# One layer of attention and state-space mixing on one core: scores over the whole array with k held twice, q's norm factor in the exponential, another order of panels

## Chip, core and metric

The kernel runs on one core of a Trainium2 chip. The metric is the device time of one execution in microseconds (us). Before the change the median of three runs is 595.13 us (594.83 to 597.0).

## What is computed

One layer of a decoder for 256 tokens of width 1024, in float32. The input is normed and multiplied with one wide matrix; its columns feed an attention branch (q, k, v, 16 heads of 64) and a state-space branch (z, xBC, dt), each gated (g_a, g_b). A gated feed-forward part and a small last gate follow.

```
h  = rms_norm(x, ln1_g)
proj = h @ w_in
q, k, v, z, xbc, dt_raw, gate_a, gate_b = jnp.split(proj, IN_OFFSETS, axis=-1)
qh = rms_norm(split_heads(q, b_, s), q_norm_g)
kh = rms_norm(split_heads(k, b_, s), k_norm_g)
att = moba_attention(qh, kh, split_heads(v, b_, s))
y_a = att @ w_o_attn
y_b = mamba2_mixer(z, xbc, dt_raw, ...) @ w_o_ssm
x = x + (sigmoid(gate_a) * y_a + sigmoid(gate_b) * y_b) @ w_out
g_ff, u_ff = jnp.split(rms_norm(x, ln2_g) @ w_gate_up, 2, axis=-1)
x = x + (silu(g_ff) * u_ff) @ w_down
x = x + (p @ w_ple_proj) * sigmoid(rms_norm(x, ln3_g) @ w_ple_gate)
```

With 256 tokens there is one attention block, so the attention is plain causal attention: the scores of a head are q times k over 64 dimensions, divided by 8, masked and put through a softmax. q and k are normed per head and token before that: each row is multiplied by a factor (its mean square plus epsilon, to the power -1/2) and by a gain per dimension.

## The kernel before

**Precision.** Every large product is done on TensorE in a rounded float32. Each factor is split into a rounded high part and the rest; three products (high x high, high x low, low x high) add up in PSUM. Names ending in h and l are such pairs.

**Weights.** The matrices come as one stream of 512 KB pieces. `load` (L271) starts the DMA into `raw` (5 buffers) on SP's queue, ACT rounds the piece into `wh` (4 buffers, L151), and DVE subtracts for `wl` (6 buffers, L265). L151 is a helper: all of ACT's work has this line, all matmuls have L170, all transposes L192.

**Panels.** The stream is used up in the order of the list `PANELS` (L34): each entry is 512 output columns. A `Panel` (L335; v, q, k, gb, ga, yb) has the tokens as output rows, takes two PSUM banks (`g`) and 48 products of 128x512. `Rows` (L380; xbc) and `Narrow` (L404; z) have the columns as output rows and take four banks (`gr`, pairs of a 128x512 and a 128x256 product) and two (`gn`, 96 products of 128x256). Panels share four banks of PSUM; a panel's first product into a bank waits until ACT or DVE have read what stood there. The first two panels (v) run while the input arrives; v, q and k use an input pair made at the start (`split_h`), and from `gb` on the panels use `hn`, which `norm_task` (L463) makes in four steps of two rows each on DVE and ACT (L486).

**Side tasks.** All else (transposes, scores, values, convolutions, the scan) runs between the panels' products. Tasks are generators; a `Filler` (L78) walks them as the panels are written out: after each step of a panel it lets one task that is due emit its next piece. When a task is due is told in a planner's own time by the table `LAG` (L68), in nanoseconds. So `PANELS` and `LAG` set where each piece stands in TensorE's order, and with it when the other engines are asked. Side tasks share four other banks of PSUM (`pb`).

**q and k** (`evac_qk`, L630). For each of the panel's two banks (128 tokens each) ACT squares, DVE sums per head (L640) and adds epsilon (L642), POOL raises both to -1/2 (L644), and DVE multiplies the bank by the factor into SBUF (L647), which frees it. After the delay `qk`, TensorE transposes, ACT multiplies by the gain and rounds, and DVE makes the low part (L658). The result has two heads on each block of 128 partitions.

**Scores** (`scores`, L837) take a pair of heads, eight pairs in all. Each head's product runs over its 64 partitions alone, and `halves` (L176) writes the two heads in turn, as they use different halves of the array's rows. There are twelve products a pair: for each head three of 128 columns (first 128 queries, first 128 keys) and three of 256 (the other queries, all keys). DVE adds the mask and takes the maximum, ACT takes the exponential with a scale of 0.125 and the maximum as bias, and DVE divides by the sum. `transp` (L871) transposes the probabilities, `values` (L887) multiplies them with v for two pairs at a time, always those before the newest.

Of the kernel before, what the change touches and what calls it, by code (L numbers as in the profile page):

```python
# [16 lines left out]
P = 128  # L17
T = 256
# [6 lines left out]
V_CW = 26  # L25
# [30 lines left out]
    ('ga', 1, 8736),
# [12 lines left out]
    "norm": 7560, "norm.x": 1763, "norm.k": 4255, "dt": 4000, "dt.t": 3068, "dt.e": 21098, "dt.low": 0,  # L69
    "dt.end": 1000, "xbc": 3513, "xbc.t": 2655, "xbc.end": 16932, "z": 9234, "z.t": 0, "z.end": 2000,  # L70
    "qk": 30613, "qk.t": 841, "qk.end": 1559, "v": 3285, "cb": 0, "rows": 0, "prep": 1025, "seg": 263,
    "seg.next": 4000, "out": 3075, "out.xdt": 2489, "out.end": 1108, "off": 2201, "off.end": 1168,
    "finish": 5045, "finish.ones": 8043, "sc": 0, "sc.tr": 0, "tr": 802, "tr.val": 0, "val": 1761, "val.end": 0,
    "m": 1896, "res": 7162, "ff": 609, "ff.end": 7593,
# [34 lines left out]
def tile_layer(ctx: ExitStack, tc: tile.TileContext, head, xk, pt, vec, w_dt, w_big, w_dn2, w_pp, out):  # L109
# [23 lines left out]
    def s4(shape, dt=F32):  # L133
        return sb.tile([P] + shape, dt, tag="s4", bufs=22, name=nm("s4"))
# [304 lines left out]
    eps1 = const.tile([P, 2], F32, name="eps1")  # L439

    def x_stats():
        with prio("bg"):
# [11 lines left out]
            nc.vector.tensor_scalar(eps1, ss1s, EPS / 1024, EPS * EPS, op0=ALU.mult, op1=ALU.add)  # L454

# [173 lines left out]

    def evac_qk(kind, i, pan):  # L630
        gcol = v[:, V_GQ : V_GQ + 1] if kind == "q" else v[:, V_GK : V_GK + 1]
        th = s4([4, T], F32R)
        tl = s4([4, T], F32R)
        qn = []
        with prio("ev"):
            ms = tiny([2, 8])
            for tt in range(2):
                sqr = s2([512])
                act(sqr, pan.ps[tt], AF.Square)
                nc.vector.tensor_reduce(ms[:, tt], sqr.rearrange("p (h d) -> p h d", d=64), axis=AX.X, op=ALU.add)  # L640
            for tt in range(2):
                nc.vector.tensor_scalar(ms[:, tt], ms[:, tt], 1.0 / 64, eps1[:, tt : tt + 1], op0=ALU.mult, op1=ALU.add)  # L642
            f = tiny([2, 8])
            nc.gpsimd.tensor_tensor(f.rearrange("p a b -> p (a b)"), ms.rearrange("p a b -> p (a b)"), mhalf, op=ALU.pow)  # L644
            for tt in range(2):
                q_ = s2([512])
                nc.vector.tensor_tensor(  # L647
                    q_.rearrange("p (h d) -> p h d", d=64), pan.ps[tt].rearrange("p (h d) -> p h d", d=64), bcast(f[:, tt], 64), op=ALU.mult)
                qn.append(q_)
        yield fill.now + LAG["qk"]  # L650
        for tt in range(2):
            with prio("bg"):
                pq = pb([4, P])
                for j in range(4):
                    transpose(pq[:, j], qn[tt][:, j * P : j * P + P])
                ts = slice(tt * P, tt * P + P)
                act(th[:, :, ts], pq, scale=gcol)
                stt(tl[:, :, ts], pq, gcol, th[:, :, ts].bitcast(F32), op0=ALU.mult, op1=ALU.subtract)  # L658
            yield fill.now + LAG["qk.t"]
        yield fill.now + LAG["qk.end"]  # L660
        qk_t[kind, i] = (th, tl)
# [171 lines left out]
    def attention_task():  # L833
# [3 lines left out]
        def scores(p):  # L837
            half, i = p
            (qh, ql), (kh, kl) = qk_t["q", half], qk_t["k", half]
            with prio("bg"):  # L840
# [3 lines left out]
                ps = [pb([512]) for _ in range(2)]  # L844
                halves(
                    (ps[hf][:, o], a[rows_of[hf], i, qs], b[rows_of[hf], i, ks], n == 0, n == 2)
                    for o, qs, ks in ((slice(0, P), slice(0, P), slice(0, P)), (slice(P, P + T), slice(P, T), slice(0, T)))
                    for n, (a, b) in enumerate(((qh, kh), (qh, kl), (ql, kh)))
                    for hf in range(2))
                for hf in range(2):  # L850
                    p_ = ps[hf]
                    nc.vector.tensor_tensor_reduce(
                        out=s[:, hf, 0:P], in0=p_[:, 0:P], in1=cmask[:, 1], scale=1.0, scalar=-3.0e38,
                        op0=ALU.add, op1=ALU.max, accum_out=mx[:, 2 * hf : 2 * hf + 1])
                    nc.vector.tensor_tensor_reduce(
                        out=s[:, hf, P : P + T], in0=p_[:, P : P + T], in1=cmask.rearrange("p a b -> p (a b)"), scale=1.0, scalar=-3.0e38,
                        op0=ALU.add, op1=ALU.max, accum_out=mx[:, 2 * hf + 1 : 2 * hf + 2])
# [295 lines left out]
def _layout(i):  # L1153
# [9 lines left out]
    def chunks(w, c0, k0, nk):  # L1163
# [5 lines left out]
        np.concatenate([f["q_norm_g"]] * 2)[:, None], np.concatenate([f["k_norm_g"]] * 2)[:, None],  # L1169
# [55 lines left out]
```

## Time and profile before

| | before |
|---|---|
| median of three runs | 595.13 us |
| the profiled execution | 595.48 us |
| its span, first to last instruction | 593.8 us |
| mean granted clock of TensorE | 0.999 |
| products on TensorE (PE) | 3183 |
| DMA traffic | 104.97 MB, mean 177 GB/s |

The profile is of one execution. A line of its tables names the source line, the engine, the operation and output <- inputs by the program's names; the shapes are partitions x elements, and for a matmul the size of the weights and of the moving rows. A timeline row starts with the start time and the time busy, both in us; brackets hold the idle time ahead of it on its engine and the instruction that ended it. Products are pipelined: one row's end lies behind the next row's start, so the cost of a product is the distance of starts. A count at the end (x12) joins equal rows that follow each other. In a row of groups the first number behind the bar is the busy time of all, the second the mean of one in ns, then the idle time ahead of them.

### The profile page before, as it was taken

The page shows a single profiled execution, that of the slowest core. Times are in us where ns is not written, and L with a number is a line of the kernel's source. Part 1 is how long each engine was busy: PE and PEld are TensorE (multiplying, and loading weights), DVE is VectorE, ACT ScalarE, POOL GpSimd, SP SyncE. Part 2 cuts the span into 40 slices and gives each one's busy share as a digit, 9 for nine tenths or more (in the row PEclk, how much of TensorE's full clock was granted, in tenths as well). Part 3 has the DMA queues.
Part 4 walks back from the last instruction along what each step waited for, and adds up shares of the span by engine and source line. Part 5 has one row for each costly group of instructions (what it writes and reads, how often), then busy time and mean ns, then how long its engine had stood idle before and what let it go on. Part 6 is the DMA issues. An engine that isn't in the chain of part 4 may idle for free.

```text
span 593.8 us, 8655 instructions
## 1 busy us (share of the span) xinstructions
PE 585.2 (99%) x3183; PEld 493.4 (83%) x3183; DVE 439.8 (74%) x703; ACT 340.9 (57%) x528; POOL 38.7 (7%) x44
## 2 busy tenths in 40 slices
PE   8999999999999999999999999999999999999997
PEld 7787778888899889888888888888888888888886
DVE  5696787999889999997957766666656666646464
ACT  6874566776877757655643445755445545445352
POOL 2004231000000024100000000000000000000000
PEclk9999999999999999999999999999999999999999
DMA  8957548655443333344465675555665565556521
GB/s 271 386 179 235 169 161 218 202 174 166 151 160 104 108 109 85 131 159 162 142 228 182 191 247 184 192 170 186 194 196 175 179 198 189 180 191 193 182 73 71
DMA packets 33322, 104.97 MB, mean 177 GB/s; under 512 B 3616, under 2 KB 7040, under 8 KB 33280
## 3 DMA queue, kind: packets, MB, share of 16 engines
q1 hardware_dynamic: 33280, 104.43, 54.1%
q8 instruction: 25, 0.41, 0.3%
q14 instruction: 17, 0.14, 0.1%
HBM read 103.28 MB, written 1.06 MB: 176 GB/s over the span
## 4 chain that ended last, share of the span: by engine, by line
PE 93%; ACT 2%; DMA 2%; DVE 1%; POOL 1%; issue 1%; SPq 1%; ACTq 0%
PE g L170 64%; PE gr L170 10%; PE gn L170 8%; PE pb L170 6%; PE pb L192 4%; ACT wh L151 1%; DMA raw<-in_head 1%; DMA xraw<-in_head 1%; ACT s L151 1%; POOL tiny L644 1%; DVE wl L265 1%; SPq L250 1%; DVE s L647 0%; DVE tiny L640 0%; DVE tiny L642 0%
## 5 line engine op out<-in xcount | busy, mean ns | idle before, releaser
L170 PE MATMUL g<-wh,s 128*128 128x512 f32 (+1 forms) x1188 | 374.6, 392 | 1.2 <-ACT wh L151 0.7
L265 DVE TENSOR_TENSOR wl<-raw,wh 128x1024 fp32r<-128x1024 f32 (+2 forms) x193 | 231.0, 1200 | 113.4 <-ACT wh L151 111.0
L151 ACT ACTIVATE wh<-raw 128x1024 fp32r<-128x1024 f32 (+2 forms) x193 | 200.1, 1038 | 179.6 <-PE g L170 131.1
L170 PEld LDWEIGHTS g<-wh,s 128*128 128x128 f32 x1188 | 222.5, 188 | 47.1 <-ACT wh L151 1.1
L170 PE MATMUL g<-wl,s 128*128 128x512 f32 (+1 forms) x594 | 230.5, 390 | 0.3 <-DVE wl L265 0.3
L170 PEld LDWEIGHTS g<-wl,s 128*128 128x128 f32 x594 | 111.5, 188 | 22.3 <-DVE wl L265 0.9
L170 PE MATMUL gr<-s,wh 128*128 128x512 f32 x192 | 69.1, 401 | 0.9 <-ACT s L151 0.9
L170 PE MATMUL gr<-s,wl 128*128 128x256 f32 x192 | 54.0, 281 | 0.0
L170 PE MATMUL gn<-s,wh 128*128 128x256 f32 x256 | 49.0, 288 | 0.0
L151 ACT ACTIVATE s<-pb 128x512 f32<-128x512 f32 (+3 forms) x58 | 29.0, 531 | 29.2 <-PE pb L192 16.7
L170 PEld LDWEIGHTS gr<-s,wh 128*128 128x128 f32 x192 | 36.0, 188 | 9.5 <-ACT s L151 1.5
L170 PEld LDWEIGHTS gn<-s,wh 128*128 128x128 f32 x256 | 40.2, 191 | 1.0 <-issue 0.3
L170 PE MATMUL gn<-s,wl 128*128 128x256 f32 x128 | 37.0, 289 | 0.0
L170 PEld LDWEIGHTS gr<-s,wl 128*128 128x128 f32 x192 | 36.3, 189 | 0.3
L192 PE MATMUL pb<-ident,s 128*128 128x128 f32 x206 | 33.0, 273 | 0.0
L170 PE MATMUL pb<-s,s 128*64 128x128 f32 (+5 forms) x336 | 30.9, 295 | 0.9 <-ACT s L151 0.9
L600 DVE SCALAR_TENSOR_TENSOR s<-s,vecs,s 128x255 f32<-128x255 f32 (+2 forms) x72 | 31.0, 477 | 0.0
L192 PEld LDWEIGHTS pb<-ident,s 128*128 128x128 f32 x206 | 25.7, 140 | 6.0
L170 PEld LDWEIGHTS pb<-s,s 128*64 128x64 f32 (+2 forms) x336 | 24.4, 158 | 6.7 <-issue 2.2
L710 POOL TENSOR_SCALAR_AFFINE_SELECT rr<-a_h 128x512 fp32r<-128x512 f32 x16 | 16.5, 1045 | 143.9 <-PE pb L170 137.4
L170 PEld LDWEIGHTS gn<-s,wl 128*128 128x128 f32 x128 | 24.4, 191 | 0.4
L151 ACT ACTIVATE s<-s 128x512 f32<-128x512 f32 (+2 forms) x23 | 18.6, 810 | 6.8 <-DVE s L1061 4.0
(143 smaller groups left out, 378.9 us busy)
## 6 DMA issues: line engine op xcount, KB each, us to landing
raw<-in_w_big SPq DMA_DIRECT2D x176, 512.0 KB
raw<-in_head SPq DMA_DIRECT2D x4, 512.0 KB
s<-in_xk SPq DMA_DIRECT2D x4, 512.0 KB
raw<-in_head SPq DMA_DIRECT2D x7, 256.0 KB
e1c<-e1d SPq DMA_DIRECT2D x2, 512.0 KB
raw<-in_w_pp SPq DMA_DIRECT2D x2, 512.0 KB
raw<-in_w_dn SPq DMA_DIRECT2D x2, 512.0 KB
out<-s SPq DMA_DIRECT2D x3, 256.0 KB
```

The costliest lines, as they stand in the source:

```text
L151: return nc.scalar.activation(o, i, f, **kw)
L170: ins = nc.tensor.matmul(o, lhsT, rhs, start=start, stop=stop).ins
L192: queue(nc.tensor.transpose(o, i, ident[: i.shape[0], : i.shape[0]]).ins, False)
L250: nc.sync.dma_start(dst, src)
L265: nc.vector.tensor_sub(wl, raw, wh.bitcast(F32))
L600: stt(cc[:, sft:], u[:, b, : T - sft], cw[3 - sft], cc[:, sft:], op0=ALU.mult, op1=ALU.add)
L644: nc.gpsimd.tensor_tensor(f.rearrange("p a b -> p (a b)"), ms.rearrange("p a b -> p (a b)"), mhalf, op=ALU.pow)
L710: nc.gpsimd.affine_select(r, bcast(a_h[:, c, h0 : h0 + 4].bitcast(F32), P), pattern=[[0, 4], [1, P]], compare_op=ALU.is_ge, fill=0.0, base ...
```

## The change

It has six parts.

**Scores over 128 rows.** k's transposed tiles exist twice. In one copy the 64 partitions of a pair's second head are zero, in the other those of the first, through gains padded with zeros (`vec` has one more column). A product of q's 128 partitions (both heads) with a copy then gives one head alone, and with both copies side by side as moving rows both heads come from one product. A pair takes three products of 256 columns and three of 512 in place of twelve of 128 and 256. They are no longer chained to each other by `halves`.

```diff
-                ps = [pb([512]) for _ in range(2)]
-                halves(
-                    (ps[hf][:, o], a[rows_of[hf], i, qs], b[rows_of[hf], i, ks], n == 0, n == 2)
-                    for o, qs, ks in ((slice(0, P), slice(0, P), slice(0, P)), (slice(P, P + T), slice(P, T), slice(0, T)))
-                    for n, (a, b) in enumerate(((qh, kh), (qh, kl), (ql, kh)))
-                    for hf in range(2))
+                ps = [pb([2, P]), pb([2, T])]
+                for qt in range(2):
+                    for n, (a, b) in enumerate(((qh, kh), (qh, kl), (ql, kh))):
+                        mm(ps[qt], a[:, i, qt * P : qt * P + P], b[:, i % 2, :, : qt * P + P], n == 0, n == 2)
...
-                nc.vector.tensor_scalar(mx, mx, -0.125, None, op0=ALU.mult)
-                parts = (slice(0, P), slice(P, P + T))
+                f = fq[half][:, :, 2 * i : 2 * i + 2]
+                stt(mx.rearrange("p (h q) -> p h q", h=2), mx.rearrange("p (h q) -> p h q", h=2), -1.0, f.rearrange("p q h -> p h q"), op0=ALU.mult, op1=ALU.mult)
...
-                        act(s[:, hf, sl], s[:, hf, sl], AF.Exp, scale=0.125, bias=mx[:, n : n + 1], accum_out=sm[:, n : n + 1])
+                        act(s[:, hf, sl], s[:, hf, sl], AF.Exp, scale=f[:, qt, hf : hf + 1], bias=mx[:, n : n + 1], accum_out=sm[:, n : n + 1])
```

**q's factor in the exponential.** q is not multiplied by its norm factor. ACT copies its banks to SBUF without waiting for POOL, and the factor (with the 1/8 in it, through `eps64`) is the scale of the exponential and multiplies the maximum. k is treated as before up to the transposes, which now take both token blocks of two column blocks at once, sixteen for a panel as before. Behind them k has two evictions on ACT and two on DVE where q has one of each.

```diff
+            if kind == "q":
+                f = fq[i]
+                for tt in range(2):
+                    q_ = s2([512])
+                    act(q_, pan.ps[tt])
+                    qn.append(q_)
...
+                if kind == "q":
+                    outs = [(qh[:, b2], ql[:, b2], V_GQ)]
+                else:
+                    kh, kl = s4([2, 2, T], F32R), s4([2, 2, T], F32R)
+                    kt.append((kh, kl))
+                    outs = [(kh[:, :, hf], kl[:, :, hf], V_GK + hf) for hf in range(2)]
+                for oh, ol, c in outs:
+                    act(oh, pq, scale=v[:, c : c + 1])
+                    stt(ol, pq, v[:, c : c + 1], oh.bitcast(F32), op0=ALU.mult, op1=ALU.subtract)
```

**Buffers.** The pool `s4` of 4 KB tiles has 25 buffers in place of 22.

**Order of panels.** Before: v0 v1 q0 q1 k1 k0 gb0 xbc5 xbc4 xbc1 xbc2 xbc3 xbc0 z0 z1 z2 z3 gb1 yb0 ga0 yb2 ga1 yb1 yb3. Now: v0 v1 k0 q0 q1 k1 gb0 xbc5 xbc4 xbc1 z0 xbc2 xbc0 z3 z1 z2 gb1 xbc3 ga0 yb0 ga1 yb2 yb1 yb3. The weights are packed in the same order.

**Delays.** Nearly every entry of `LAG` differs, among them the norm's and q's and k's:

```diff
-    "norm": 7560, "norm.x": 1763, "norm.k": 4255, "dt": 4000, "dt.t": 3068, "dt.e": 21098, "dt.low": 0,
+    "norm": 7506, "norm.x": 8000, "norm.k": 3650, "dt": 5547, "dt.t": 2000, "dt.e": 28229, "dt.low": 1915,
```

The longer `norm.x` moves the norm's last two rows (L486, now L488). On DVE they stood between the square sums of the third panel; they now stand behind five evictions of q and k (L681), among them k's first column blocks.

**Where instructions stand.** Order of TensorE, the second pair of heads, before: `pb_1597` and `pb_1598` are the two heads' banks, behind the arrow stands the moving input and then the weights: `s_150` and `s_151` are k's high and low part, `s_72` and `s_73` q's. `gr` is a panel of xbc.

```order
L170 MATMUL pb_1597<-s_150_794,s_72_451 128x128
L170 MATMUL gr_1445<-s_38_209,wh_1544 128x512
...
L170 MATMUL gr_1447<-s_38_209,wl_1545 128x256
L170 MATMUL pb_1598<-s_150_794,s_72_451 128x128
L170 MATMUL pb_1597<-s_151_795,s_72_451 128x128
L170 MATMUL pb_1598<-s_151_795,s_72_451 128x128
...
L170 MATMUL pb_1597<-s_150_794,s_73_452 128x256
L170 MATMUL pb_1598<-s_150_794,s_73_452 128x256
L170 MATMUL gr_1448<-s_38_209,wh_1544 128x512
```

The same engine, the first pair of heads, now: `s_139` and `s_140` are k's high and low part, both copies side by side, `s_141` and `s_142` q's. The two rows of `pb_1456` ahead are another task's.

```order
L170 MATMUL gr_1496<-s_35_207,wh_1500 128x512
L170 MATMUL pb_1456<-s_177_922,s_205_1066 128x256
L170 MATMUL pb_1456<-s_177_922,s_205_1066 128x128
L170 MATMUL pb_1471<-s_139_746,s_141_752 128x256
L170 MATMUL pb_1471<-s_140_747,s_141_752 128x256
L170 MATMUL pb_1471<-s_139_746,s_142_753 128x256
L170 MATMUL pb_1472<-s_139_746,s_141_752 128x512
L170 MATMUL pb_1472<-s_140_747,s_141_752 128x512
L170 MATMUL pb_1472<-s_139_746,s_142_753 128x512
L170 MATMUL gr_1496<-s_35_207,wl_1501 128x256
```

Twelve products, of which the first stood alone ahead of a stretch of the panel, are six. Here they stand together; in some later pairs panel work stands between the three narrow and the three wide ones.

TensorE where the first panel of xbc follows gb0, before: `g_159` is gb0's second bank, `gr_177` to `gr_180` are the banks of xbc5, and `gr_178` is the one that waits for gb0's second bank to be read. `pb_187` is dt's.

```order
L170 MATMUL g_159_812<-wh_170_856,s4_38_209 128x512
L170 MATMUL gr_177_904<-s4_35_206,wh_182_909 128x512
L170 MATMUL gr_177_904<-s4_35_206,wl_183_910 128x256
L170 MATMUL gr_177_904<-s4_35_206,wh_182_909 128x512
L170 MATMUL gr_177_904<-s4_35_206,wl_183_910 128x256
L170 MATMUL pb_187_924<-a_l_213,gt_r_94 128x64
L170 MATMUL pb_187_924<-a_h_212,gt_r_94 128x32
L170 MATMUL pb_187_924<-le_r_95,a_h_212 32x128
L170 MATMUL pb_187_924<-le_r_95,a_l_213 32x128
L170 MATMUL gr_178_905<-s4_35_206,wh_182_909 128x512
```

The same place now: gb0's second bank is `g_149`, xbc5's banks are `gr_179` to `gr_182`, and the one behind it is `gr_182`, the fourth.

```order
L170 MATMUL g_149_784<-wh_163_837,s4_38_210 128x512
L170 MATMUL gr_179_924<-s4_35_207,wh_184_929 128x512
L170 MATMUL gr_179_924<-s4_35_207,wl_185_930 128x256
L192 MATMUL pb_168_872<-ident_83,s2_166_854 128x128 x2
...
L170 MATMUL gr_181_926<-s4_35_207,wl_185_930 128x256
L192 MATMUL pb_189_952<-ident_83,s2_136_737 128x128
L192 MATMUL pb_189_952<-ident_83,s2_137_739 128x128
L192 MATMUL pb_189_952<-ident_83,s2_136_737 128x128
L192 MATMUL pb_189_952<-ident_83,s2_137_739 128x128
L170 MATMUL gr_182_927<-s4_35_207,wh_184_929 128x512
```

The bank that gb0 frees last was opened behind one block of xbc5, and is now opened behind three blocks and six transposes.

TensorE at the second `values`, before: `pb_385` and `pb_386` are the banks of a pair's transposed probabilities, `pb_388` that of `values`, whose first product waits for ACT.

```order
L170 MATMUL gn_391_2117<-s4_38_209,wl_412_2230 128x256
L192 MATMUL pb_385_2071<-ident_83,s4_368_1924 128x128 x2
L192 MATMUL pb_386_2072<-ident_83,s4_368_1924 128x128
L192 MATMUL pb_385_2071<-ident_83,s4_368_1924 128x128 x2
L192 MATMUL pb_386_2072<-ident_83,s4_368_1924 128x128
L170 MATMUL pb_388_2102<-s4_349_1835,s4_53_340 64x256 x2
L170 MATMUL pb_388_2102<-s4_349_1835,s4_53_340 64x128 x2
```

Now (`pb_394` is `values`):

```order
L192 MATMUL pb_382_2066<-ident_83,s4_365_1923 128x128
L170 MATMUL gn_387_2087<-s4_37_209,wl_405_2193 128x256
...
L192 MATMUL pb_382_2066<-ident_83,s4_365_1923 128x128
L192 MATMUL pb_383_2067<-ident_83,s4_365_1923 128x128
L192 MATMUL pb_382_2066<-ident_83,s4_365_1923 128x128 x2
L192 MATMUL pb_383_2067<-ident_83,s4_365_1923 128x128
L170 MATMUL pb_394_2130<-s4_346_1824,s4_55_344 64x256 x2
```

It still stands behind six transposes, the first of which now comes earlier, but its first product waits for nothing on ACT any more.

The vector and scalar instructions follow the same two tables; no other code of the kernel changed.

More of the change, by code (lines that the diff above doesn't have):

```diff
@@ L36 @@
     ('v', 1, 2560),
+    ('k', 0, 1024),
     ('q', 0, 0),
@@ L68 @@
 LAG = {
-    "norm": 7560, "norm.x": 1763, "norm.k": 4255, "dt": 4000, "dt.t": 3068, "dt.e": 21098, "dt.low": 0,
[L70 to L74, printed above, removed]
+    "norm": 7506, "norm.x": 8000, "norm.k": 3650, "dt": 5547, "dt.t": 2000, "dt.e": 28229, "dt.low": 1915,
+    "dt.end": 2412, "xbc": 3526, "xbc.t": 6309, "xbc.end": 16627, "z": 3649, "z.t": 182, "z.end": 637,
+    "qk": 20242, "qk.t": 841, "qk.end": 2494, "v": 0, "cb": 1128, "rows": 26, "prep": 1000, "seg": 556,
+    "seg.next": 8000, "out": 5850, "out.xdt": 0, "out.end": 1000, "off": 959, "off.end": 144, "finish": 1889,
+    "finish.ones": 10266, "sc": 0, "sc.tr": 261, "tr": 2065, "tr.val": 139, "val": 1056, "val.end": 255,
+    "m": 3510, "res": 3942, "ff": 137, "ff.end": 3573,
 }
@@ L439, in tile_layer @@
     eps1 = const.tile([P, 2], F32, name="eps1")
+    eps64 = const.tile([P, 2], F32, name="eps64")
     def x_stats():
@@ L628, in rows_z @@
         return after, end
+    fq = [const.tile([P, 2, 8], F32, name=nm("fq")) for _ in range(2)]
     def evac_qk(kind, i, pan):
-        gcol = v[:, V_GQ : V_GQ + 1] if kind == "q" else v[:, V_GK : V_GK + 1]
-        th = s4([4, T], F32R)
-        tl = s4([4, T], F32R)
         qn = []
@@ L640, in evac_qk @@
                 nc.vector.tensor_reduce(ms[:, tt], sqr.rearrange("p (h d) -> p h d", d=64), axis=AX.X, op=ALU.add)
+            if kind == "q":
[5 more added lines that the diff above has]
+            else:
+                f = tiny([2, 8])
             for tt in range(2):
[L642 removed]
@@ L643, in evac_qk @@
-            f = tiny([2, 8])
+                if kind == "q":
+                    nc.vector.tensor_scalar(ms[:, tt], ms[:, tt], eps64[:, tt : tt + 1], None, op0=ALU.add)
+                else:
+                    nc.vector.tensor_scalar(ms[:, tt], ms[:, tt], 1.0 / 64, eps1[:, tt : tt + 1], op0=ALU.mult, op1=ALU.add)
             nc.gpsimd.tensor_tensor(f.rearrange("p a b -> p (a b)"), ms.rearrange("p a b -> p (a b)"), mhalf, op=ALU.pow)
[L645 to L649, printed above, removed]
@@ L650, in evac_qk @@
-        yield fill.now + LAG["qk"]
-        for tt in range(2):
-            with prio("bg"):
[L653 to L658, printed above, removed]
+            if kind == "k":
+                for tt in range(2):
+                    q_ = s2([512])
+                    nc.vector.tensor_tensor(
+                        q_.rearrange("p (h d) -> p h d", d=64), pan.ps[tt].rearrange("p (h d) -> p h d", d=64), bcast(f[:, tt], 64), op=ALU.mult)
+                    qn.append(q_)
@@ new lines, in evac_qk @@
+        yield fill.now + LAG["qk"]
+        qh, ql, kt = [], [], []
+        if kind == "q":
+            qh, ql = s4([4, T], F32R), s4([4, T], F32R)
+        for jj in range(2):
+            b2 = slice(2 * jj, 2 * jj + 2)
+            with prio("bg"):
+                pq = pb([2, T])
+                for j in range(2):
+                    for tt in range(2):
+                        transpose(pq[:, j, tt * P : tt * P + P], qn[tt][:, (2 * jj + j) * P : (2 * jj + j) * P + P])
+                if kind == "q":
+                    outs = [(qh[:, b2], ql[:, b2], V_GQ)]
+                else:
+                    kh, kl = s4([2, 2, T], F32R), s4([2, 2, T], F32R)
[4 more added lines that the diff above has]
+                    stt(ol, pq, v[:, c : c + 1], oh.bitcast(F32), op0=ALU.mult, op1=ALU.subtract)
```

34 lines of the change are left out of this document (16 added, 18 removed).

## The prediction

> **What bounds the kernel now.** I read the page from the top: the busy times, then the chain that ended last.
>
> ```profile
> span 593.8 us, 8655 instructions
> PE 585.2 (99%) x3183; PEld 493.4 (83%) x3183; DVE 439.8 (74%) x703; ACT 340.9 (57%) x528; POOL 38.7 (7%) x44
> PE 93%; ACT 2%; DMA 2%; DVE 1%; POOL 1%; issue 1%; SPq 1%; ACTq 0%
> ```
>
> TensorE (PE) is busy 585.2 of 593.8 us and is 93% of the chain. A change can therefore save in two ways only: less work on PE, or fewer of its waits. The stages show where the waits are (columns: stretch, length, then busy time and count of PE, PEld, DVE, ACT, POOL, granted clock, DMA share, GB/s).
>
> ```profile
> 17.00:100.00 83.00, 81.46 (x398) 66.96 (x398) 63.72 (x106) 51.52 (x81) 17.71 (x9) 1.00 0.68 220
> 100.00:250.00 150.00, 148.97 (x1097) 132.64 (x1096) 142.16 (x302) 107.94 (x211) 12.27 (x11) 1.00 0.44 140
> 250.00:580.00 330.00, 330.00 (x1573) 273.25 (x1573) 217.91 (x267) 167.38 (x215) 4.96 (x7) 1.00 0.56 181
> ```
>
> From 250 us on PE never stops, and the change touches nothing there. PE is idle 83.00 - 81.46 = 1.54 us in the first row and 150.00 - 148.97 = 1.03 us in the second: together 2.57 us, the whole store of waits that the change can reach. In the second row VectorE (DVE) is busy 142.16 of 150 us, 95%: this is the engine that is next behind PE. The granted clock is 1.00, so it is no part of the argument.
>
> **Scores: what they cost on PE.** A group of twelve half-height products that stands alone:
>
> ```profile
> 145.41 0.40 PE L170 MATMUL gr<-s,wh 128*128 128x512 f32 x1
> 145.65 0.28 PE L170 MATMUL gr<-s,wl 128*128 128x256 f32 x1
> 145.77 0.39 PE L170 MATMUL gr<-s,wh 128*128 128x512 f32 x1
> 146.09 0.96 PE L170 MATMUL pb<-s,s 64*128 64x128 f32 x12
> 146.98 0.39 PE L170 MATMUL gr<-s,wl 128*128 128x256 f32 x1
> 147.20 0.40 PE L170 MATMUL gr<-s,wh 128*128 128x512 f32 x1
> ```
>
> A duration in a row overlaps the next instruction, so I go by starts. One wh and one wl product take 145.77 - 145.41 = 0.36 us (0.24 and 0.12). With the twelve in between the same two take 147.20 - 145.77 = 1.43 us, so the group costs 1.07 us: 146.98 - 146.09 = 0.89 of its own, the rest (0.18) where 128-row and 64-row products meet. Three of the eight groups look like this. The other five are cut in two by panel work:
>
> ```profile
> 174.60 0.40 PE L170 MATMUL gn<-s,wh 128*128 128x256 f32 x2
> 174.93 0.32 PE L170 MATMUL pb<-s,s 64*128 64x128 f32 x1
> 175.18 0.39 PE L170 MATMUL gn<-s,wl 128*128 128x256 f32 x1
> 175.40 0.40 PE L170 MATMUL gn<-s,wh 128*128 128x256 f32 x2
> 175.64 0.28 PE L170 MATMUL gn<-s,wl 128*128 128x256 f32 x1
> 175.85 0.96 PE L170 MATMUL pb<-s,s 64*128 64x128 f32 x11
> 176.73 0.51 PE L170 MATMUL gn<-s,wh 128*128 128x256 f32 x2
> 177.07 0.29 PE L170 MATMUL gn<-s,wl 128*128 128x256 f32 x1
> ...
> 147.65 0.32 PE L170 MATMUL pb<-s,s 64*128 64x128 f32 x1
> ...
> 211.72 0.32 PE L170 MATMUL pb<-s,s 64*128 64x128 f32 x1
> ```
>
> A 128x256 product takes 0.12 us (175.40 to 175.64 holds two). From 174.60 to 177.07 are 2.47 us with eight of them, 0.96, so this group costs 1.51 us. (The last two rows are the first and the last of the five lone first products.) All scores together: 3 x 1.07 + 5 x 1.51 = 10.8 us.
>
> After, a pair is three 128x256 and three 128x512 products with all 128 rows in use. That they meet whole-height neighbours free of charge is seen where transposes stand inside a panel:
>
> ```profile
> 376.13 0.39 PE L170 MATMUL g<-wh,s 128*128 128x512 f32 x1
> 376.36 0.60 PE L192 MATMUL pb<-ident,s 128*128 128x128 f32 x4
> 376.71 0.48 PE L170 MATMUL g<-wh,s 128*128 128x512 f32 x1
> 377.03 0.40 PE L170 MATMUL g<-wl,s 128*128 128x512 f32 x1
> ```
>
> From 376.36 to 377.03 are 0.67 us for four transposes and one 128x512 product; the product is 0.23 (376.13 to 376.36), leaving 0.11 for each transpose, which is also their distance inside a long run of them. So a pair costs 3 x 0.12 + 3 x 0.23 = 1.05 us, eight cost 8.4, and the term is 8.4 - 10.8 = **-2.4 us**. Its bounds: 0 if every piece of the saving were a cost of entering side work at all, and -2.4 - 8 x 0.1 = -3.2 if the neighbours of the old groups lost more than the rows show.
>
> [...]
>
> **The other engines.**
>
> ```profile
> L151 ACT ACTIVATE s<-pb 128x512 fp32r<-128x512 f32 x19 | 11.1, 597 | 21.1 <-PE pb L192 15.6 <-PE pb L170 5.5
> L151 ACT ACTIVATE s<-pb,vecs 128x512 fp32r<-128x512 f32 x8 | 5.5, 686 | 4.0 <-PE pb L192 4.0
> L658 DVE SCALAR_TENSOR_TENSOR s<-pb,vecs,s 128x512 fp32r<-128x512 f32 x8 | 6.0, 747 | 0.8 <-ACT s L151 0.8
> L647 DVE TENSOR_TENSOR s<-g,tiny 128x512 f32<-128x512 f32 x8 | 5.1, 685 | 3.8 <-POOL tiny L644 3.8
> ```
>
> DVE loses four products for q (4 x 0.685 = 2.7 us) and gains four second evictions of k (4 x 0.747 = 3.0) and one tiny multiplication: +0.3 us. ScalarE (ACT) gains four copies of q's banks (4 x 0.60 = 2.4 us), four evictions of k (4 x 0.69 = 2.7) and the scale of 32 exponentials read from a tile (0.686 - 0.597 = 0.09 each by the first two rows, 0 to 2.9 us in all). ACT is busy 51.52 of 83 and 107.94 of 150 us, which is the cover for these 5 to 8 us; without it they would delay the rounding of weights one for one. POOL, the DMA queue and the weight stream keep their work; the weights only come in another order. The three more buffers stand against k's tiles, four more of which live until the last scores.
>
> **The waits.** All but 0.30 us of the 2.57 us is in four rows, which I take with their causes.
>
> ```profile
> 46.18 3.97 POOL L644 TENSOR_TENSOR tiny<-tiny,mhalf 128x16 f32<-128x16 f32 x1 [20.08 <-DVE tiny L642]
> 50.18 1.29 DVE L647 TENSOR_TENSOR s<-g,tiny 128x512 f32<-128x512 f32 x2 [2.80 <-POOL tiny L644]
> 51.02 0.47 PE L170 MATMUL g<-wh,s 128*128 128x512 f32 x1 [0.56 <-DVE s L647]
> ...
> 87.15 0.39 PE L170 MATMUL gr<-s,wh 128*128 128x512 f32 x1
> 88.32 0.58 ACT L151 ACTIVATE s<-g 128x512 f32<-128x512 f32 x1
> 88.95 0.50 PE L170 MATMUL gr<-s,wh 128*128 128x512 f32 x1 [0.68 <-ACT s L151]
> ...
> 115.21 0.50 PE L170 MATMUL gr<-s,wh 128*128 128x512 f32 x1 [0.17 <-ACT s L151]
> 195.89 0.82 PE L192 MATMUL pb<-ident,s 128*128 128x128 f32 x6
> 197.56 0.65 PE L170 MATMUL pb<-s,s 128*64 128x256 f32 x4 [0.86 <-ACT s L151]
> ```
>
> At 51.02 PE waits for q0's bank: POOL's power takes 3.97 us, and only then DVE can multiply it out. The new q needs no power there, but k0 now stands in third place and keeps that chain. I take -0.2 (0 if the chain is as long as it was, -0.56 at best). At 88.95 PE waits for the second bank of gb0. The panel ended at 87.15, and the bank's tanh, which stands behind two weight roundings on ACT, ends at 88.32 + 0.58 = 88.90, 1.75 us later. PE was there at 88.95 - 0.68 = 88.27, 1.12 us after the panel, behind one block of the next panel and four short products. In the new order that bank is the fourth that the next panel opens, behind three blocks (twice 0.36 each) and six transposes: 3 x 0.72 + 6 x 0.11 = 2.8 us, so the wait goes: **-0.7**. The wait at 115.21 is a row panel's bank behind another row panel; the order has 3 such neighbours in place of 5: **-0.2**. At 197.56 the second values stand right behind six transposes and wait for an ACT copy. In the new order that wait on ACT is gone from these products: **-0.9**. What is late next after each is the same engine's next bank or weights, and that is the fifth term: a new order of panels and delays makes waits of its own. From nothing to what the old order shows in these rows (2.3 us); I take **+0.7**, nearer to nothing, since banks come free with 1 us to spare at the places I followed, and the xbc panels, whose convolution is DVE's work, no longer stand six in a row.
>
> **The sum** against the profiled execution: -2.4 - 0.2 - 0.7 - 0.2 - 0.9 + 0.7 = -3.7 us, 595.5 - 3.7 = 591.8. That execution took 595.48 us, 0.35 above the median of the runs (595.13), so in the frame of the median 591.4.
>
> **The rivals.**
>
> A, the sum. With all its bounds at their low ends (scores -3.2, the wait at 51 us -0.56, no new waits) it is 589.5; with 2.3 us of new waits 593.0.
>
> B, waits move and do not go. The scores come out as computed, but xbc's evictions, DVE at 95% and buffers held longer give back 2.3 to 4.5 us of new waits instead of 0.7. For it: four tiles of k live on, and some products now stand 3 us behind their producers. Against it: 25 buffers instead of 22. 593.0 to 595.2, about 594.
>
> C, the six full products are no cheaper. The old group's own 0.89 us becomes 1.05, +1.3 us over eight, and what neighbours lose (0.18, or 0.62 where cut) stays because any strange group costs it. Against it: the transposes above. Then +1.3 - 2.0 + 0.7 = 0.0: about 595.
>
> [...]
>
> D, slower: the last rows of the normed input come late.
>
> ```profile
> 40.96 0.87 DVE L486 SCALAR_TENSOR_TENSOR s<-xraw,x,s 128x256 fp32r<-128x256 f32 x2
> ```
>
> They are ready at 42 us today and first needed by gb0, 18 products before its end at 87.15: 87.15 - 18 x 0.23 = 83.0. The new delays put them behind five evictions of k and q on DVE, which wait for sixteen transposes about the end of the sixth panel (48 products earlier than gb0's end: 76.1). If nothing overlaps they come at 76.1 + 16 x 0.11 + 5 x 0.75 + 0.87 = 82.5. Beyond 83.0 each microsecond is one on PE. It decides the sign when they are 6.7 us late, which takes POOL's power (3.97) and more than one of the evictions' own length again ahead of them. About 599.
>
> **How the numbers follow.** A 0.60, B 0.25, C 0.08, D 0.07. The prediction is A's, 591.4. The range starts at A's low end and reaches over B to C: 589.5 to 595.5. Half a per cent, about what a measurement of this kernel can tell from no change, is 3.0 us, so faster means under 592.1: nearly all of A, 0.53. Within it lie the rest of A, B and C, 0.39. Slower (over 598.1) is D and the open end of B: 0.08.
>
> **What would show it.** Right: 48 score products of 128 rows in place of 96 of 64, groups of six that cost 1.05 us from neighbour to neighbour, PE idle below 1.5 us between 17 and 250 us, no wait at gb0's bank or at the second values, ACT up by 5 to 8 us, DVE unchanged within 1 us. Wrong: groups over 1.3 us (C), PE waits in 17 to 250 us that still add up to 2.5 us or more (B), a wait on DVE's norm rows in gb0 (D).

## The result and the profile after

| | before | changed |
|---|---|---|
| median | 595.29 us (4 runs) | 590.52 us (4 runs, 589.85 to 590.67) |
| ratio | 1 | 0.9913, 95% interval 0.9891 to 0.9934 |
| span of the profiled execution | 593.8 us | 588.6 us |

The change takes 4.8 us off, where 3.7 were forecast; 590.52 lies inside the range, 0.9 us under the predicted 591.4. The page after:

```profile
span 588.6 us, 8563 instructions
PE 582.4 (99%) x3135; PEld 494.0 (84%) x3135; DVE 438.4 (74%) x704; ACT 347.0 (59%) x536; POOL 36.9 (6%) x44
PE 93%; DVE 3%; DMA 2%; ACT 1%; SPq 1%; issue 0%; ACTq 0%
```

TensorE has 48 products fewer and 2.8 us less work (582.4 for 585.2). ACT is up by 6.1 us, inside the 5 to 8 of the prediction. DVE is down by 1.4, where it was to be unchanged within 1 us; the same forms under the old tables add 0.3 (e2 below: 440.1), as worked out, so the rest came with the order, and why is not shown. The stages after, in the columns of the prediction's table, with the head of the program ahead of them:

```profile
0.00:17.00 17.00, 15.84 (x67) 13.35 (x67) 9.25 (x21) 11.12 (x19) 3.87 (x17) 1.00 0.89 294
17.00:100.00 83.00, 82.95 (x411) 68.93 (x410) 63.87 (x101) 57.91 (x89) 12.34 (x5) 1.00 0.64 216
100.00:250.00 150.00, 149.31 (x1060) 135.02 (x1059) 139.50 (x300) 108.77 (x210) 13.86 (x15) 1.00 0.48 149
```

PE's idle time is 0.05 and 0.69 us where it was 1.54 and 1.03. So the span's 5.2 us are 2.8 of work, 1.8 of waits (2.57 to 0.74) and 0.6 at the head, whose idle time fell from 1.80 (17.00 - 15.20) to 1.16. That last part cannot be put down to the change: over the twelve kernels below the head idles 1.1 to 2.3 us. The same holds for 0.30 of the waits, a single one at 17.31 us for a weight's low part: e4 and e5, which leave the order of that stretch as it was, do not have it either. What the change took from the waits is 1.5 us.

A pair's scores after, from TensorE's timeline:

```profile
177.30 0.28 PE L170 MATMUL gn<-s,wl 128*128 128x256 f32 x1
177.42 0.52 PE L170 MATMUL pb<-s,s 128*128 128x256 f32 x3
177.78 0.40 PE L170 MATMUL gn<-s,wh 128*128 128x256 f32 x2
178.02 0.28 PE L170 MATMUL gn<-s,wl 128*128 128x256 f32 x1
178.14 0.86 PE L170 MATMUL pb<-s,s 128*128 128x512 f32 x3
178.84 0.40 PE L170 MATMUL gn<-s,wh 128*128 128x256 f32 x2
```

The three narrow products take 177.78 - 177.42 = 0.36 us and the three wide ones 178.84 - 178.14 = 0.70, together 1.06. This pair is cut in two by panel work and pays nothing for it: the neighbours keep their 0.12 (177.30 to 177.42).

The four old waits are gone. At gb0's second bank (ACT's and PE's timeline) the tanh is ready at 88.03 + 0.58 = 88.61, and PE opens the bank at 89.48, right behind the last four of the six transposes:

```profile
88.03 0.58 ACT L151 ACTIVATE s<-g 128x512 f32<-128x512 f32 x1
...
89.13 0.60 PE L192 MATMUL pb<-ident,s 128*128 128x128 f32 x4
89.48 0.48 PE L170 MATMUL gr<-s,wh 128*128 128x512 f32 x1
```

One new wait has come. On DVE's timeline the product that frees z0's second bank (L624) stands behind a weight split, and PE waits for it at the row panel that follows z0:

```profile
136.62 1.21 DVE L265 TENSOR_TENSOR wl<-raw,wh 128x1024 fp32r<-128x1024 f32 x1
137.76 0.67 DVE L624 SCALAR_TENSOR_TENSOR s<-s,gn 128x512 f32<-128x512 f32 x1
...
138.48 0.50 PE L170 MATMUL gr<-s,wh 128*128 128x512 f32 x1 [0.69 <-DVE s L624]
```

### The profile page after: what moved, and what is told of

The parts are those of the page before. It is cut to its first block, busy times and chain, and to the rows that moved or that the text cites. A ratio compares the mean times of both kernels' runs of the same rounds, so it can differ in the third digit from the quotient of the medians.

```text
span 588.6 us, 8563 instructions
## 1 busy us (share of the span) xinstructions
PE 582.4 (99%) x3135; PEld 494.0 (84%) x3135; DVE 438.4 (74%) x704; ACT 347.0 (59%) x536; POOL 36.9 (6%) x44
## 3 DMA queue, kind: packets, MB, share of 16 engines
HBM read 103.28 MB, written 1.06 MB: 177 GB/s over the span
## 4 chain that ended last, share of the span: by engine, by line
PE 93%; DVE 3%; DMA 2%; ACT 1%; SPq 1%; issue 0%; ACTq 0%
PE g L170 67%; PE gr L170 11%; PE pb L170 6%; PE gn L170 6%; PE pb L192 4%; DVE wl L265 1%; DMA raw<-in_head 1%; DMA xraw<-in_head 1%; DVE s L602 1%; SPq L250 1%; ACT wh L151 0%; DVE s L598 0%; DVE s L624 0%; ACT s L151 0%; DVE s L1165 0%
## 5 line engine op out<-in xcount | busy, mean ns | idle before, releaser
L602 DVE SCALAR_TENSOR_TENSOR s<-s,vecs,s 128x255 f32<-128x255 f32 (+2 forms) x72 | 33.1, 501 | 0.0
L170 PE MATMUL pb<-s,s 128*64 128x128 f32 (+4 forms) x288 | 31.5, 302 | 0.0
L170 PEld LDWEIGHTS pb<-s,s 128*64 128x64 f32 (+1 forms) x288 | 24.8, 154 | 4.4 <-issue 1.8
L733 POOL TENSOR_SCALAR_AFFINE_SELECT rr<-a_h 128x512 fp32r<-128x512 f32 x16 | 14.1, 898 | 156.4 <-PE pb L170 124.2
```

Source lines behind the costliest of these rows:

```text
L170: ins = nc.tensor.matmul(o, lhsT, rhs, start=start, stop=stop).ins
L602: stt(cc[:, sft:], u[:, b, : T - sft], cw[3 - sft], cc[:, sft:], op0=ALU.mult, op1=ALU.add)
L733: nc.gpsimd.affine_select(r, bcast(a_h[:, c, h0 : h0 + 4].bitcast(F32), P), pattern=[[0, 4], [1, P]], compare_op=ALU.is_ge, fill=0.0, base ...
```

## The experiments

Each kernel was timed beside the kernel before, on the same chip; the ratio is to that kernel. The first four take the change apart.

**e1, the scores alone.** The full-height forms and the doubled k, with q multiplied on DVE as before, in the old order of panels with the old delays. The planner's time for a group is set back to the old one. Against the changed kernel:

```diff
- PANELS, LAG of the change
+ PANELS, LAG of before
-            if kind == "q":
-                f = fq[i]
...
+                fill.now = t0_ + 648.0
...
-                        act(s[:, hf, sl], s[:, hf, sl], AF.Exp, scale=f[:, qt, hf : hf + 1], ...)
+                        act(s[:, hf, sl], s[:, hf, sl], AF.Exp, scale=0.125, ...)
```

> The kernel before with one part of the change alone: k held twice and six full-height score products for a pair; q still multiplied by its factor on DVE, panels and delays of before (the planner is told the old duration, so that the order stays), 25 buffers. Theory 1 (half of the gain is TensorE's own work in the scores): eight groups at 1.06 us in place of 10.9 us in all, so 2.4 us less, about 592.8, and the four waits of before (0.56, 0.68, 0.17, 0.86 us) are still there. Theory 2 (the scores gave nothing, all of the gain is waits): 595.2 within 0.4.

Measured: 598.81 us, ratio 1.0052 (1.0037 to 1.0066): slower by 3.5 us, where both theories had it at about 595.2 or less. The profiled execution is the fastest of the five (597.62). TensorE's timeline, DVE's behind it, and the stages around the end of the wait:

```profile
187.84 0.86 PE L170 MATMUL pb<-s,s 128*128 128x512 f32 x3
188.54 0.60 PE L192 MATMUL pb<-ident,s 128*128 128x128 f32 x4
188.89 0.49 PE L170 MATMUL gn<-s,wh 128*128 128x256 f32 x2
...
191.70 1.22 PE L170 MATMUL pb<-s,s 128*128 128x256 f32 x6
197.01 0.45 PE L192 MATMUL pb<-ident,s 128*128 128x128 f32 x1 [4.10 <-DVE s L876]
197.62 1.30 PE L192 MATMUL pb<-ident,s 128*128 128x128 f32 x5 [0.16 <-DVE s L876]
198.85 0.69 PE L170 MATMUL pb<-s,s 128*64 128x256 f32 x2
...
192.74 0.16 DVE L869 TENSOR_SCALAR tiny<-tiny 128x4 f32<-128x4 f32 x1
193.21 1.21 DVE L265 TENSOR_TENSOR wl<-raw,wh 128x1024 fp32r<-128x1024 f32 x1
196.24 0.17 DVE L874 RECIPROCAL tiny<-tiny 128x4 f32<-128x4 f32 x1
196.44 1.03 DVE L876 TENSOR_TENSOR s<-s,tiny 128x256 f32<-128x256 f32 x2
...
195.00:200.00 5.00, 2.83 (x14) 1.88 (x16) 4.40 (x17) 3.58 (x11) 0.00 (x0) 0.69 0.33 113
200.00:205.00 5.00, 5.00 (x43) 4.49 (x40) 4.80 (x15) 2.30 (x7) 0.00 (x0) 0.97 0.01 3
```

Behind the next pair's six products stand the transposes of the pair before, and these wait 4.10 us for its softmax: DVE makes the exponential's bias only at 192.74 and divides at 196.44, with convolution taps, a weight split and the next pair's maxima between. But the softmax is no slower than before; its transposes stand elsewhere. In the kernel before, the pair at this place has its scores on TensorE and its division on DVE at these times:

```profile
185.95 0.96 PE L170 MATMUL pb<-s,s 64*128 64x128 f32 x11
194.64 1.03 DVE L866 TENSOR_TENSOR s<-s,tiny 128x256 f32<-128x256 f32 x2
```

The scores end at 185.95 + 0.89 = 186.84 there and at 187.84 + 0.70 = 188.54 in e1, so the division starts 7.8 us behind them before and 7.9 in e1. TensorE came to the transposes at 195.89 before, 9.05 us behind the scores with panel products in between; in e1 it comes at 197.01 - 4.10 = 192.91, after 4.37 us. The same tables gave another order, although the planner was told the old duration, and why they did is not shown. So e1 prices the new products with the places that the old tables give them, not in the old order of instructions. A wait of 0.99 us at 102 us, in place of the 0.17 at 115, adds to it.

The wait costs twice: the granted clock (the third number from the end) is 0.69 in the five microseconds in which it ends and 0.97 in the next five. Five transposes behind the wait take 198.85 - 197.62 = 1.23 us, 0.25 each; four ahead of it take 188.89 - 188.54 = 0.35, 0.09 each.

Two more waits of over 4 us show it. In e2, which waits 4.5 us at the same place, the granted clock is 0.86 from 195 to 200 us and 0.80 from 200 to 205; in e12 it is 0.67 in the five microseconds behind a wait of 6.05 us. Around one of 3.15 us in a profiled execution (e8) it is 1.00 from 250 to 260 us. No run has a wait between 3.15 and 4.10 us.

**e2, both forms.** As e1, but with q's factor in the exponential: the changed kernel with the old panels and delays.

```diff
- PANELS, LAG of the change
+ PANELS, LAG of before
```

> The change with the panels and delays of before: full-height scores and q's factor in the exponential. Theory 1: as the scores alone, and the wait at 51 us (0.56) goes too, since q's banks are copied without POOL: about 592.3. Theory 2: 595.2 less the one wait, 594.6.

Measured: 599.20 us, 1.0061 (1.0048 to 1.0074), above both theories (592.3 and 594.6). The same place waits again, as the table of PE's waits has it (us in total, times, longest):

```profile
PE pb L192 <- ACT s L151: 4.5, 1, 4.5
```
The wait at the third panel's bank is gone, as expected, but it is gone in e1 too, where q still needs POOL and the power took 2.91 us; e5 shows why.

**e3, the order alone.** The kernel before with the new panels, delays and 25 buffers, half-height scores and q multiplied on DVE. The planner's time for a group is that of the change.

```diff
- PANELS, LAG of before
+ PANELS, LAG of the change
-        return sb.tile([P] + shape, dt, tag="s4", bufs=22, name=nm("s4"))
+        return sb.tile([P] + shape, dt, tag="s4", bufs=25, name=nm("s4"))
...
+                fill.now = t0_ + 960.0
```

> The kernel before with the new panel order, the new delays and 25 buffers alone (half-height scores, q multiplied on DVE; the planner is told the new scores' duration). Theory 1: the old waits (2.27 us) go and the one at z0's bank (0.7) comes, -1.6; and only 2 of the 8 score groups are cut in this order in place of 5, 3 x 0.44 = -1.3: about 592.3. Theory 2 (half-height scores cost the same wherever they stand): 593.6. Theory 3 (the order's gain needs the new q): waits of 0.5 us or more at the third panel's bank.

Measured: 591.45 us, 0.9929 (0.9915 to 0.9943): 3.8 us of the gain without the new forms. Its stages:

```profile
17.00:100.00 83.00, 83.00 (x412) 68.99 (x411) 64.13 (x104) 53.56 (x80) 12.33 (x5) 1.00 0.64 216
100.00:250.00 150.00, 150.00 (x1103) 133.25 (x1102) 139.72 (x295) 105.50 (x209) 13.33 (x15) 1.00 0.46 148
```

PE never stops here: all 2.57 us of waits went, the 0.30 at 17.31 among them, and none came. Two of the eight score groups are cut, which saves 3 x 0.44 = 1.3. The 2.27 us of the four waits and these 1.3 are 3.6 of the 3.8 us. Theory 1 holds but for the wait at z0's bank, which does not come without the new forms.

**e4, groups kept whole.** The kernel before with a product of 64 columns ahead of each group:

```diff
-    def halves(products):
+    def halves(products, first=None):
...
-        last = None
+        last = first
...
-                halves(
+                tie = mm(ps[1][:, 0:64], qh[:, i, 0:P], kh[:, i, 0:64], True, True)
+                fill.now -= 107.0
+                halves((
...
-                    for hf in range(2))
+                    for hf in range(2)), tie)
```

> The kernel before with one product more ahead of each group of scores (128 rows, 64 columns, into the second head's bank, overwritten afterwards), which holds the first half-height product back until both banks are free, so that no group is cut; all else as before. Theory 1 (a cut group costs 0.44 us more because half-height products meet full-height ones twice and the first runs without its partner): 5 x 0.44 less and 8 x 0.05 more, -1.8, about 593.4, groups at 1.07 us. Theory 2 (a half-height group costs what it costs, cut or not): 595.6.

Measured: 593.91 us, 0.9972 (0.9961 to 0.9984), -1.35. In the timeline no group is cut any more:

```profile
173.56 0.20 PE L170 MATMUL pb<-s,s 128*128 128x64 f32 x1
173.59 0.48 PE L170 MATMUL gn<-s,wh 128*128 128x256 f32 x2
173.91 0.28 PE L170 MATMUL gn<-s,wl 128*128 128x256 f32 x1
174.12 0.96 PE L170 MATMUL pb<-s,s 64*128 64x128 f32 x12
175.01 0.51 PE L170 MATMUL gn<-s,wh 128*128 128x256 f32 x2
175.35 0.29 PE L170 MATMUL gn<-s,wl 128*128 128x256 f32 x1
```

The added product costs 0.03 + 0.08 us (173.59 to 173.91 is 0.32 for what takes 0.24), 0.9 at most for eight where the expectation had 0.05 each, against 5 x 0.44 = 2.2 saved: -1.3, as measured. Theory 1 holds, with a dearer added product. So 2.2 of the 2.4 us that the scores were to bring are the price of cutting half-height groups, which an order without cuts saves just as well.

**e5, POOL ahead of the split.** The kernel before with one idle operation of 8 columns on DVE, and no other change in any engine's order:

```diff
+            if (kind, i) == ("q", 0):
+                idle = tiny([2, 32])
+                gap.append(nc.vector.tensor_scalar(idle[:, 0, 0:8], ms[:, 1], 1.0, None, op0=ALU.mult).ins)
...
+            if loads[0] == 6:
+                follow(low, gap[0])
```

> The kernel before with one idle tiny DVE operation (128x8) between the last epsilon of q0 and the weight split that follows it; the order of all engines is otherwise that of before. In the two runs with a wait at the third panel's bank DVE's split starts 0.02 us before POOL's power, and the power takes 3.97 us; in the four without it the power starts first or alone and takes 2.9. Theory 1 (the split, once begun, keeps POOL out for the rest of it): the power now starts first, takes 2.9, the wait of 0.56 goes to nothing, about 594.7. Theory 2 (the first power is long for another reason): 3.97 again, the same wait, 595.3.

Measured: 594.16 us, 0.9982 (0.9974 to 0.9991), that is 0.5 to 1.5 us less; the expected 0.56 lies at the edge. DVE's and POOL's timelines:

```profile
45.17 0.17 DVE L651 TENSOR_SCALAR tiny<-tiny 128x8 f32<-128x8 f32 x1
45.25 1.26 DVE L267 TENSOR_TENSOR wl<-raw,wh 128x1024 fp32r<-128x1024 f32 x1
...
45.22 2.90 POOL L653 TENSOR_TENSOR tiny<-tiny,mhalf 128x16 f32<-128x16 f32 x1 [20.00 <-DVE tiny L648]
```

The power starts 0.03 us ahead of the split and takes 2.90 us, not 3.97, and the wait is gone, as theory 1 has it; what holds a power behind a split back is not shown. An operation more made the kernel faster, and in the trace the order of every engine is otherwise that of before. In the kernel before the split started first, by 0.02 us:

```profile
46.16 1.23 DVE L265 TENSOR_TENSOR wl<-raw,wh 128x1024 fp32r<-128x1024 f32 x1
```

A power behind a split is longer by 3.97 - 2.90 = 1.07 us, nearly the whole split of 1.23; a split that starts while the power runs is not held back: here it takes 1.26 us inside the power's 2.90. Of the 56 powers of this shape in the fourteen traces three (before, e4, e11) take 3.97, in before and e4 with a split 0.02 us ahead; the others take 2.90 or 2.91, and splits that start beside them 1.22 (before) to 1.29 (e1, e2).

**e6, z0's bank freed by ACT.** The changed kernel; ACT copies z0's banks, and DVE's product reads the copy:

```diff
+                src = ps
+                if i == 0:
+                    src = s2([2, T])
+                    act(src, ps)
                 act(zz, ps, AF.Tanh, scale=0.5)
-                stt(zz, zz, 1.0, ps, op0=ALU.add, op1=ALU.mult)
+                stt(zz, zz, 1.0, src, op0=ALU.add, op1=ALU.mult)
```

> The change, with z0's two banks copied to SBUF by ACT, so that DVE's product (which stands behind the convolution's backlog) no longer frees them. Theory 1: the only wait left between 17 and 580 us (0.69, at z0's second bank) goes, 0.7 less than the change, 589.8. Theory 2 (the backlog of DVE only moves the wait to the next bank or weight): as the change, 590.5.

Measured: 591.76 us, 0.9940 (0.9927 to 0.9954): 1.2 us more than the change, with intervals that just overlap. No gain is shown, and the wait grew. ACT's timeline, then PE's:

```profile
137.66 0.28 ACT L151 ACTIVATE s<-pb 128x128 f32<-128x128 f32 x1 [3.95 <-DVE s L722]
137.83 1.08 ACT L151 ACTIVATE s<-gn 128x512 f32<-128x512 f32 x2
...
138.97 0.50 PE L170 MATMUL gr<-s,wh 128*128 128x512 f32 x1 [1.83 <-ACT s L151]
```

ACT's copy of the bank stands behind a small copy that itself waited 3.95 us for DVE (L722, behind the convolution). Neither theory had this: the backlog reached the bank through another queue. The copy is not the only difference, either: in the trace TensorE, DVE and ACT have other orders from about 133 us on, the first pair's scores among them (they begin at 139.77 us in place of 142.47).

**e7, q's factor back in q.** The changed kernel with q multiplied on DVE and a scale of 0.125.

```diff
-            if kind == "q":
-                f = fq[i]
...
-            if kind == "k":
+            if True:
                 for tt in range(2):
...
-                        act(s[:, hf, sl], s[:, hf, sl], AF.Exp, scale=f[:, qt, hf : hf + 1], ...)
+                        act(s[:, hf, sl], s[:, hf, sl], AF.Exp, scale=0.125, ...)
```

> The change without one part: q is multiplied by its factor on DVE as before, and the exponential's scale is 0.125. Theory 1 (the factor's place takes no part in the gain, since k stands third and no wait hangs on q's banks): 590.5 within 0.5, PE idle between 17 and 250 us within 0.5 of 0.74. Theory 2 (q's banks behind POOL's power are late again): a wait of 0.5 to 1 us at the panels after q0 or q1, 591 to 592.

Measured: 590.37 us, 0.9910 (0.9897 to 0.9923); PE idles 0.03 and 0.67 us in the two stages. Theory 1: no effect of this part is shown, in the waits (0.74 us in the change) or in the time, though the intervals of the two kernels leave room for 1.5 us either way.

**e8, transposes due later.** The kernel of e2 with one delay changed:

```diff
-    "sc": 0, "sc.tr": 0, "tr": 802,
+    "sc": 0, "sc.tr": 12000, "tr": 802,
```

> The kernel of e2 (full-height scores and q's factor in the exponential with the panels and delays of before) with one delay longer: transposes of the probabilities are due 12 us after the scores instead of at once. In e2 they stood 4 to 5 us behind their scores on TensorE at one place and waited 4.5 us there for the softmax; now the smallest distance is 13 us. Theory 1 (the old delays are what made the forms slower): that wait goes, 599.2 - 4.7 = 594.5, less if the 1.0 us wait at 101 us goes too. Theory 2 (the second evictions of k on ACT and DVE make the forms slower): 597 or more, in other waits.

Measured: 599.47 us, 1.0059 (1.0043 to 1.0076). The wait for the softmax is gone, as theory 1 says, but `values` now waits at 256 us for ACT's copies of transposes:

```profile
256.13 1.30 PE L170 MATMUL pb<-s,s 128*64 128x256 f32 x12 [3.15 <-ACT s L151]
```

Theory 1 named the first wait rightly and the time wrongly: one delay moved alone only moved the wait. Theory 2 had the time (597 or more, in other waits), but its cause, k's second evictions, does not stand at this wait: in the 3 us ahead of it ACT rounds weights and works on other tiles. The wait of 0.94 us at 102 us stays as well. The profiled execution took 596.6 us at a granted clock of 0.998, the other five 598.7 to 600.0 at 0.994 to 0.995.

**e9, z0's product ahead of the split.** The changed kernel, with the two DVE rows shown under the result exchanged (the fourth weight split behind z0's product is told to follow it).

```diff
-                stt(zz, zz, 1.0, ps, op0=ALU.add, op1=ALU.mult)
+                low = stt(zz, zz, 1.0, ps, op0=ALU.add, op1=ALU.mult).ins
+                if i == 0 and jj == 1:
+                    gap.append(low)
...
+            if loads[0] == 4:
+                follow(low, gap[0])
```

> The change, with z0's second product on DVE told to stand ahead of the weight split before which it stood behind (one pair swapped on DVE; later parts of the order shift a little). Theory 1 (that split of 1.2 us is what makes the bank late): the wait of 0.69 us goes, PE idle between 17 and 250 us under 0.2, 589.8. Theory 2 (the slot is only taken by the next one in DVE's backlog, or the split is late for its own panel): a wait of 0.5 or more stays or comes, 590.5.

Measured: 590.37 us, 0.9923 (0.9908 to 0.9939). The table of PE's waits:

```profile
PE g L170 <- ACT s L151: 0.4, 1, 0.4
PE g L170 <- DVE wl L267: 0.2, 1, 0.2
```

The wait of 0.69 is gone and two of 0.4 and 0.2 us stand elsewhere. No gain over the change is shown: theory 2, with smaller pieces. More than the two rows moved: in the trace the scores of the first pair, too, stand later on TensorE, so the exchange is not tested alone.

**e10, the delays alone.** The kernel before with the new `LAG` and 25 buffers, old panels.

```diff
- LAG of before
+ LAG of the change
```

> The kernel before with the new delays (and 25 buffers) and its own panel order. Theory 1 (the delays carry the gain of the new order, since three of the four waits are side tasks' places): waits at 51, 88 and 197 us gone or under 0.3 each, about 592.5. Theory 2 (the panel order carries it): 594.5 or more.

Measured: 598.34 us, 1.0054 (1.0039 to 1.0068). PE idles 4.36 us from 100 to 250. The longest wait is at a row panel of xbc:

```profile
140.12 0.50 PE L170 MATMUL gr<-s,wh 128*128 128x512 f32 x1 [2.42 <-ACT s L151]
```

**e11, the panels alone.** The kernel before with the new `PANELS` and 25 buffers, old delays.

```diff
- PANELS of before
+ PANELS of the change
```

> The kernel before with the new panel order (and 25 buffers) and its own delays. Theory 1 (the delays carry the gain): waits of 1.5 us or more remain between 17 and 250 us, 594 or more. Theory 2 (the panel order carries it): 592 to 593.

Measured: 595.40 us, 1.0000 (0.9991 to 1.0010). PE idles 1.24 us from 17 to 100 (the waits at the third panel's bank and at gb0 are there) and 0.18 from 100 to 250. That is 1.15 us less than before, which the median does not show; TensorE's busy time is 586.1 us for 585.2, and why is not shown. The two expectations of e10 and e11 both took one table to carry the gain; neither does.

**e12, the change with the old panels.** New forms and delays, old `PANELS`.

```diff
- PANELS of the change
+ PANELS of before
```

> The change with the old panel order: new forms, new delays. Theory 1 (the new forms need the new delays, not the new panels; the smallest distance from scores to their transposes on TensorE is 10.9 us here, as in the change, where it was 3.8 with the old delays): no wait over 1.5 us for the softmax, at most 593. Theory 2 (they need the panels too): a wait of 3 us or more and 595 or more.

Measured: 597.63 us, 1.0048 (1.0035 to 1.0062). No wait for the softmax is left, but one of 6.05 us at the place of e10. PE's timeline, ACT's, and the stages:

```profile
142.46 0.79 PE L170 MATMUL gr<-s,wh 128*128 128x512 f32 x1 [6.05 <-ACT s L151]
...
141.65 0.28 ACT L151 ACTIVATE s<-pb 128x128 f32<-128x128 f32 x1 [2.84 <-DVE s L718]
141.82 1.08 ACT L151 ACTIVATE s<-gr 128x512 f32<-128x512 f32 x2
...
136.00:143.00 7.00, 0.95 (x4) 0.69 (x4) 6.44 (x16) 2.41 (x6) 0.00 (x0) 0.75 0.63 229
143.00:148.00 5.00, 5.00 (x22) 4.34 (x21) 3.96 (x8) 3.05 (x5) 0.00 (x0) 0.67 0.00 0
```

Here a row panel follows a row panel. ACT must copy the first one's banks, and that copy stands behind the same small copy as in e6, which waits for DVE's convolution backlog. In the new panel order z0 stands at this place; ACT reads its banks (tanh) ahead of the small copy, and only DVE's product is late, by 0.69 us. The delays put the small copy there; the panels make it harmless. Theory 2 holds: the new forms need the panels too, though not against the wait for the softmax.

## Why the prediction was right, point by point

**The bound.** TensorE's own work and its waits between 17 and 250 us made the difference: 2.8 + 1.5 of 5.2 us in the profiled executions. The other 0.9 (0.6 in the head, 0.3 in the wait at 17.31) come and go in kernels that change nothing there.

**Scores, -2.4.** The sizes held: 1.06 us for a group where 1.05 was worked out, whether it is cut or not, so rival C falls. All of PE's work fell by 2.8; the other 0.4 us are less than one execution's busy time differs from another's with the same products in the same order (e5: 584.6 for 585.2). What the term did not say is that it belongs to two causes. Most of it is the price of cut groups, which an order with fewer cuts also removes (e3, e4); on top of the new order the forms bring 0.9 us by the medians (591.45 to 590.52). The intervals of the two ratios overlap, so this part is likely and not shown; two cut groups fewer (2 x 0.44) would make it.

**Waits, -0.2 - 0.7 - 0.2 - 0.9.** Those at 88, 115 and 197 us went as worked out; at gb0 TensorE came to the bank 89.48 - 86.82 = 2.66 us after the panel's end, where 2.8 was forecast. The step that failed is the first: "The new q needs no power there, but k0 now stands in third place and keeps that chain. I take -0.2". The chain stayed, but the power took 2.90 us and not 3.97:

```profile
45.88 2.90 POOL L655 TENSOR_TENSOR tiny<-tiny,mhalf 128x16 f32<-128x16 f32 x1 [19.46 <-DVE tiny L654]
48.81 1.29 DVE L659 TENSOR_TENSOR s<-g,tiny 128x512 f32<-128x512 f32 x2 [1.33 <-POOL tiny L655]
```

so PE did not wait at all, -0.56. The 3.97 was read as the power's duration, though the three other powers of that kernel take 2.90; in e5 a start 0.03 us ahead of the weight split, where it had been 0.02 us behind, made the difference of 1.07 us. k0 in third place does not by itself free the chain: with the old delays (e11) the power again took 3.97 us and TensorE waited 0.6 for the bank.

**New waits, +0.7.** One of 0.69 us came, at z0's bank. The size was right by luck of the choice within 0 to 2.3; the argument for it ("banks come free with 1 us to spare") did not hold at z0's bank, the one place that waits.

**Rival B** (waits move) did not come in the change but is what most of the experiments met: e1, e2, e6, e8, e10 and e12 each have waits in other places, up to 6.05 us.

**Rival D** is refuted with room: the norm's last rows end at 78.58 + 0.87 = 79.45 us, and PE comes for them 18 products before gb0's end, at 86.82 - 18 x 0.23 = 82.7.

```profile
78.58 0.87 DVE L488 SCALAR_TENSOR_TENSOR s<-xraw,x,s 128x256 fp32r<-128x256 f32 x2
```

They were worked out for 82.5, with nothing overlapping.

**The sum as a sum.** With what each of its terms measured it is -2.4 - 0.56 - 0.68 - 0.17 - 0.86 + 0.74 = -3.9 us, near the -3.7 that was forecast: the size missed at the third panel (0.36) is most of the difference. For the 0.9 us beyond it (4.8 by the medians) no cause is shown; between the two profiled executions it is the head and the wait at 17.31. But the parts, run alone, do not add up: scores under the old tables +3.5 us (e1), the delays alone +3.0 (e10), the panels alone nothing (e11), delays and panels -3.8 (e3), all -4.8. The terms were read from the new order as a whole, and are shown only for it.

## What to carry to other kernels

An order tuned for one set of durations and queue entries is part of the kernel: judge a new form of a product with an order made for it, or a wait that the old tables make hides what it brings. Look, too, at where the instructions really stand: in e1, e6 and e9 more moved than the edit names. The half-height products here cost most where they were cut from their partners (1.51 us a group); kept together (1.07) they cost what six full-height ones do (1.06). Before a wait is explained by an operation's duration, look at that operation's other occurrences: the power that takes 3.97 us once takes 2.9 at the three other places of the same kernel, and what sets the one apart is a weight split that started 0.02 us ahead of it.

## What was not expected of the hardware

A power of 16 columns on POOL took 2.90 us, and 3.97 where a weight split on DVE started 0.02 us ahead of it (before, e4). Started first, the power kept its 2.90 (e5) or 2.91 (e1), and the split beside it took 1.26 and 1.29 us, where one with no power beside it takes 1.22 (before, 51.39 us).

A long stop of TensorE cost more than its length. After 4.10 us of waiting (e1) the granted clock was 0.69 from 195 to 200 us, and a transpose behind the wait took 0.25 us, where one ahead of it took 0.09. Around the wait of 6.05 us (e12) it was 0.75 from 136 to 143 us, 0.67 over the 5 us behind that and 1.00 from 148 to 153; a 128x512 product behind the wait took 143.69 - 143.27 = 0.42 us, one ahead of it 135.48 - 135.25 = 0.23. Around a wait of 3.15 us (e8, profiled) it stayed at 1.00.
